# An overflowing expert searched and loaded inside the passes, and the rotary embedding ahead of the norms

## The chip, the core and the metric

The program runs on one core of one Trainium2 chip. A core has TensorE (matmul), VectorE, ScalarE, GpSimd and SyncE, which run side by side and wait for one another by semaphores, and 16 DMA engines, which bring data from HBM to the on-chip memory SBUF. TensorE writes to eight PSUM banks. The metric is device microseconds of one execution; lower is better. All data is float32. [...]

## The reference

256 tokens of width 1024 go through two blocks. The first block has two attentions over one projection and a feed-forward layer. What matters here is its second attention, where queries and keys of 96 per head (64 plain, 32 rotary) are normed and then rotated:

```python
c_q, c_kv, k_rope = ...                       # from proj = rms_norm(x) @ w_in
qb = (rms_norm(c_q, cq_norm_g) @ w_uq).reshape(b, s, 8, 96)
kv = (rms_norm(c_kv, ckv_norm_g) @ w_ukv).reshape(b, s, 8, 128)
kb = concatenate([kv[..., :64], broadcast(k_rope)], -1)
qb, kb = rms_norm(qb, qnorm_b_g), rms_norm(kb, knorm_b_g)
qb = concatenate([qb[..., :64], apply_rope(qb[..., 64:], positions)], -1)   # kb likewise
```

The second block has two layers; each ends with a mixture of 32 experts (1024 to 128 to 1024, gate, up and down), of which every token takes two, and a gated embedding:

```python
hid = silu(einsum('td,edf->tef', xt, w_gate)) * einsum('td,edf->tef', xt, w_up)
y = einsum('tef,efd->td', hid * cw[:, :, None], w_down)    # cw: two non-zero weights for a token
h = h + y
h = h + sigmoid(rms_norm(h, ln_ple) @ ple_w_gate) * (p @ ple_w_proj)
```

Which experts a token takes depends on the data.

## The kernel before

**Weights.** `Stream` loads all weights in the order of use into an arena of 21 buffers of 1 MB (`NB`), on SyncE's queue. `W.room(n)` leaves n buffers to other data; `pump` emits loads while fewer than 21 - n are held and a whole buffer is free; `W.drop` gives one back and pumps. SyncE and TensorE run in the order of the program; VectorE, ScalarE and GpSimd have their orders made by a scheduler, separately inside and outside each branch or loop. A DMA waits on its issuing engine until the one that used the same of eight DMA semaphores before it has landed.

**Products.** Most products are three passes over halves: `split` makes a high part (ScalarE, sometimes GpSimd) and a low part (VectorE, sometimes GpSimd) of each weight, and `mm3` issues three matmuls. In `proj` the split of the next two steps stands ahead of the matmuls, in a ring of five buffers.

**Experts.** In `moe`, eight passes (`q` from 0 to 7, here passes one to eight) take four experts each. Each expert has 32 slots (`CAP`); `pick` makes the selection table `d` of a pass, `gather` collects the tokens, `gate_up`, `hidden`, `turn` and `down` compute, `combine` adds to `acc`. Gate and up are two loads of 0.5 MB for an expert, down one load for two experts. Before pass seven stands the projection of the gated embedding (`ple_proj`). Tokens beyond 32 of an expert are a job: `njob` counts them, and `overflow`, behind pass eight, runs a loop over the jobs inside a branch. In the loop VectorE finds the expert (`top`, `ei`), ScalarE loads the table `c_place` and then the expert's weights by a register, VectorE makes `R.d`, and TensorE gathers and computes up to 112 tokens (`MORE`). In this data the first layer has one job and the second none.

**Second attention of the first block.** The order on TensorE is `cq` (two halves), `ckv`, `qa`, `uq` (two halves), `ukv`, `ka`, `va`, then the transposes `heads_T` to `qTb` and `kTb`. What is made of a product's result (`cq_done`, `ckv_done`, `uq_done`, `ukv_done`, `qkv_done`) is put in `late` and runs two splits into the next product. Behind `ukv` VectorE takes one reciprocal root for q and k together, GpSimd multiplies q by it, and `rope` rotates q and k for each half of the tokens with six VectorE operations; its temporaries come from the ring `sq` of five buffers, which `head_ss` and others share.

**Start.** SyncE issues the identity, `x` in four pieces and the first weights; ScalarE issues `small` (all gains). `Rstd.add` squares a quarter of `h` on ScalarE, and its result `r` is first used in `ckv_done`.

Of the kernel before, what the change touches and what calls it, by code (L numbers as in the profile page):

```python
# [251 lines left out]
def block_kernel(ctx, tc, I, out):  # L252
# [499 lines left out]
    def rope(dst1, dst2, x1, x2, w, t, nh, eng):  # L752
        sh = [128, nh, 16]
        tb = [rt[:, w, i, t].unsqueeze(1).to_broadcast(sh) for i in range(4)]
        uvzy = sq2("ru")[:, 0:64 * nh].rearrange("p (a h d) -> p a h d", a=4, h=nh)
        u, v, z, y = [uvzy[:, i] for i in range(4)]
        eng.tensor_tensor(u, x1, tb[0], OP.mult)
        eng.tensor_tensor(v, x2, tb[1], OP.mult)
        eng.tensor_tensor(z, x2, tb[2], OP.mult)
        eng.tensor_tensor(y, x1, tb[3], OP.mult)  # L760
        eng.tensor_tensor(dst1, u, v, OP.subtract)
        eng.tensor_tensor(dst2, z, y, OP.add)
# [105 lines left out]
    def moe(l, router, rs):  # L868
# [195 lines left out]
        def overflow(T):  # L1064

            gu, dn = take("ovg", [2, 1024]), take("ovd", [1024])
            R = Step(new_d(128), T)
            n = nc.values_load(njob_i[0:1, 0:1], min_val=0, max_val=32)
            with tc.If(n > 0):
                with tc.For_i(0, n, 1):  # L1070
                    tmp = sq2("job")
                    key, hot, cwh = tmp[:, 0:32], tmp[:, 32:64], tmp[:, 64:128].rearrange("p (t q e) -> p t q e", t=2, q=8)
                    top, cnt, keyj = tmp[:, 128:129], tmp[:, 129:130], tmp[:, 130:134].rearrange("p (t a) -> p t a", t=2)
                    wj, place, ei = tmp[:, 134:138].rearrange("p (t a) -> p t a", t=2), tmp[:, 256:384], tmp[:, 138:139]
                    wr = new_d(4)
                    nc.scalar.dma_start(place, I["c_place"])
                    ebase = C("ebase")[:, 0:32]
                    V.tensor_scalar(key, ebase, float(S), None, OP.add)
                    V.scalar_tensor_tensor(hot, jobs, 0.5, key, OP.is_gt, OP.mult)
                    V.tensor_reduce(top, hot, AX.X, OP.max)  # L1080
                    V.tensor_scalar(ei.bitcast(I32), top, 1.0 / S, -1.0, OP.mult, OP.add)
                    e = nc.values_load(ei.bitcast(I32)[0:1, 0:1], engines=(ENG.Activation,), min_val=0, max_val=31)
                    for a, src in enumerate((I["moe_w_gate_2"], I["moe_w_up_2"])):
                        nc.scalar.dma_start(gu[:, a].unsqueeze(1), src[l, bass.ds(e, 1)].rearrange("e (p k) f -> p e (k f)", k=8))
                    nc.scalar.dma_start(dn.unsqueeze(1), I["moe_w_down_2"][l, bass.ds(e, 1)].rearrange("e p n -> p e n"))
                    V.tensor_scalar(hot, key, top, None, OP.is_equal)
                    V.tensor_tensor(key, jobs, hot, OP.mult)
                    V.tensor_reduce(cnt, key, AX.X, OP.add)
                    V.tensor_tensor(jobs, jobs, hot, OP.subtract)

                    V.tensor_scalar(cnt, cnt, float(MORE), float(CAP - MORE + 1 - S), OP.mult, OP.add)
                    V.tensor_tensor(cnt, cnt, top, OP.add)
                    V.tensor_scalar(keyj, k8[:, :, 0:2], cnt, None, OP.subtract)
                    for t in range(2):
                        V.tensor_scalar(R.d[:, t], place, keyj[:, t, 0:1], None, OP.is_equal)
                        V.scalar_tensor_tensor(R.d[:, t], place, keyj[:, t, 1:2], R.d[:, t].bitcast(F32),
                                               OP.is_equal, OP.add)
                    for t in range(2):
                        V.tensor_tensor(cwh[:, t], cw[:, t, :, 0:4], hot.rearrange("p (q e) -> p q e", q=8), OP.mult)
                        V.tensor_reduce(wj[:, t, 0:1], cwh[:, t].rearrange("p q e -> p (q e)"), AX.X, OP.add)  # L1100
                        V.tensor_copy(wj[:, t, 1:2], cw[:, t, 0, 4:5])
                    A.copy(wr[:, :, 0:2], wj)
                    V.tensor_tensor(wr[:, :, 2:4], wj, wr[:, :, 0:2].bitcast(F32), OP.subtract)
                    drain(gather(R.d, [R], R.banks))
                    b = R.bank("ex")
                    for t in range(2):
                        nc.tensor.transpose(b[:, t * 128:(t + 1) * 128], R.d[:, t].bitcast(F32), ident)
                    for t in range(2):
                        mm(b[:, 256:260], R.d[:, t], wr[:, t], start=t == 0, stop=t == 1)
                    A.copy(R.d, b[:, 0:256].rearrange("p (t n) -> p t n", t=2))  # L1110
                    A.copy(R.ej[:, 0], b[:, 256:260])
                    V.tensor_tensor(R.cs, R.ej[:, 0, 0:2], R.ej[:, 0, 2:4], OP.add)
                    V.tensor_scalar(R.cs[:, 0:1], R.cs[:, 0:1], 0.5, None, OP.mult)
                    b = R.gu()
                    for k in range(8):
                        mm(b[:, 0:256], R.xe[:, k], gu[:, :, k * 128:(k + 1) * 128], start=k == 0, stop=k == 7)
                    hidden(R)
                    turn(R)
                    for c in range(2):
                        b = R.bank(f"y{c}")  # L1120
                        mm(b, R.hT, dn[:, c * 512:(c + 1) * 512], start=True, stop=True)
                        A.copy(R.yd[c][:, 0], b)
                        V.tensor_tensor(R.yd[c][:, 1], b, R.yd[c][:, 0].bitcast(F32), OP.subtract)
                    combine(R, False)
            drop("ovg", "ovd")
# [3 lines left out]
        for q in range(8):  # L1129
# [49 lines left out]
        def squares():  # L1179
            for c in range(2):  # L1180
# [75 lines left out]
    for c in range(2):  # L1256
        for t in range(2):
            rs.add(c, t)
# [786 lines left out]
```

## Time and profile before

| | us |
|---|---|
| median of 3 runs | 874.78 (874.02 to 875.28) |
| the profiled execution | 876.18 |
| its span, first to last instruction | 874.4 |
| TensorE busy in it | 824.1 |
| VectorE, ScalarE, GpSimd busy | 520.4, 446.3, 226.0 |

All rows below are of the one profiled execution, with times from the start of its span. PE is TensorE, PEld its loading of the stationary operand, DVE VectorE, ACT ScalarE, POOL GpSimd, SP SyncE; a q behind a name means the engine's sequencer. L995 is line 995 of the kernel. A line of the timeline has start, duration, engine, line, operation, what is written and read, how many, and in brackets the idle time of the engine before it with what ended it.

### The profile page before, as it was taken

To read this page: it belongs to the slowest core of one execution; us is meant where nothing else is said; L and a number is where in the kernel's file an instruction comes from. 1 tells how busy PE (TensorE), PEld (TensorE's weight loads), DVE (VectorE), ACT (ScalarE), POOL (GpSimd) and SP (SyncE) were. 2 spreads that over 40 slices of the span, in tenths; PEclk is the share of its full clock that TensorE was granted. 3 is DMA by queue.
4 is the path that set the end of the run, shared out by engine and by line. 5 is a ranking of instruction groups with operands and counts; after the bars stand their busy time and mean duration, and the time that the engine had idled before them with its cause. 6 is when DMAs were issued, how large, how long until landed. Compare 5 with 4: busy or idle time off the path is not lost. (4 is left out here: it accounts for less than half of the span.)

```text
span 874.4 us, 15706 instructions
## 1 busy us (share of the span) xinstructions
PE 824.1 (94%) x5660; PEld 643.5 (74%) x5660; DVE 520.4 (60%) x1501; ACT 446.3 (51%) x1084; POOL 226.0 (26%) x293
## 2 busy tenths in 40 slices
PE   8997999999999999999899999955899899999997
PEld 5995878999999988686667666625587678666656
DVE  5669666755454567679864644321688875543355
ACT  6675865644444456367764133410676764232463
POOL 2225452222222234314554100000122455000011
PEclk9999999999999999999999999995999899999999
DMA  9991329655556542446024799999363615799971
GB/s 309 385 376 36 128 89 398 241 183 169 197 188 191 193 154 97 147 155 239 4 88 165 284 390 405 408 395 379 133 217 123 221 63 192 285 384 406 408 276 49
DMA packets 85136, 200.04 MB, mean 229 GB/s; under 512 B 5776, under 2 KB 27584, under 8 KB 85056
## 3 DMA queue, kind: packets, MB, share of 16 engines
q1 hardware_dynamic: 82704, 195.61, 61.6%
q10 hardware_dynamic: 2352, 3.40, 1.2%
q8 instruction: 46, 0.75, 0.4%
q14 instruction: 34, 0.28, 0.1%
HBM read 197.93 MB, written 1.06 MB: 228 GB/s over the span
## 5 line engine op out<-in xcount | busy, mean ns | idle before, releaser
L537 DVE TENSOR_TENSOR s<-a,s 128x512 fp32r<-128x512 f32 (+3 forms) x281 | 189.6, 685 | 127.0 <-ACT s L536 92.8
L536 ACT CAST s<-a 128x512 fp32r<-128x512 f32 (+3 forms) x294 | 172.6, 599 | 169.7 <-PE pj L543 71.5
L541 PE MATMUL pj<-s,a 128*128 128x512 f32 (+3 forms) x456 | 176.1, 386 | 4.5 <-ACT a L518 2.9
L542 PE MATMUL pj<-s,a 128*128 128x512 f32 (+3 forms) x456 | 170.6, 374 | 5.5 <-DVE s L537 5.4
L543 PE MATMUL pj<-s,a 128*128 128x512 f32 (+3 forms) x456 | 170.7, 374 | 1.3 <-DVE a L519 1.2
L537 POOL TENSOR_TENSOR s<-a,s 128x512 fp32r<-128x512 f32 (+3 forms) x71 | 90.4, 1273 | 302.8 <-ACT s L536 247.1
L541 PEld LDWEIGHTS pj<-s,a 128*128 128x128 f32 x456 | 86.4, 190 | 23.6 <-issue 5.6
L534 POOL TENSOR_SCALAR s<-a 128x512 fp32r<-128x512 f32 (+3 forms) x58 | 40.5, 698 | 243.0 <-PE pj L543 120.4
L542 PEld LDWEIGHTS pj<-s,a 128*128 128x128 f32 x456 | 86.7, 190 | 19.7 <-DVE s L537 7.4
L543 PEld LDWEIGHTS pj<-s,a 128*128 128x128 f32 x456 | 86.6, 190 | 18.2 <-DVE a L519 3.6
L1517 PE MATMUL f<-a,s 128*128 128x256 f32 x256 | 72.7, 284 | 0.0
L1519 PE MATMUL f<-a,s 128*128 128x256 f32 x256 | 72.4, 283 | 0.0
L1518 PE MATMUL f<-a,s 128*128 128x256 f32 x256 | 72.4, 283 | 0.0
L1027 PE MATMUL gu<-a,xe 128*32 128x256 f32 x1024 | 58.7, 380 | 0.6 <-DVE xe L1002 0.6
L1027 PEld LDWEIGHTS gu<-a,xe 128*32 128x32 f32 x1024 | 32.6, 110 | 28.3 <-issue 4.8
L541 PE MATMUL acc<-s,a 128*128 128x512 f32 x128 | 50.1, 391 | 0.0
L542 PE MATMUL acc<-s,a 128*128 128x512 f32 x128 | 49.9, 390 | 0.0
L543 PE MATMUL acc<-s,a 128*128 128x512 f32 x128 | 49.8, 389 | 0.0
L1517 PEld LDWEIGHTS f<-a,s 128*128 128x128 f32 x256 | 49.1, 192 | 0.2
L1518 PEld LDWEIGHTS f<-a,s 128*128 128x128 f32 x256 | 49.1, 192 | 0.2
L1519 PEld LDWEIGHTS f<-a,s 128*128 128x128 f32 x256 | 49.1, 192 | 0.0
L638 POOL TENSOR_SCALAR P<-P,nd 128x128 f32<-128x128 f32 x64 | 30.9, 495 | 50.8 <-DVE nd L633 18.3
(365 smaller groups left out, 1414.6 us busy)
## 6 DMA issues: line engine op xcount, KB each, us to landing
a<-in_w_ff_dram SPq DMA_DIRECT2D x32, 1024.0 KB, 5.6
a<-in_moe_w_gate_dram SPq DMA_DIRECT2D x64, 512.0 KB, 7.0
a<-in_moe_w_up_dram SPq DMA_DIRECT2D x64, 512.0 KB, 8.2
a<-in_moe_w_down_dram SPq DMA_DIRECT2D x32, 1024.0 KB, 9.2
a<-in_a_w_in_dram SPq DMA_DIRECT2D x10, 1024.0 KB, 5.1
a<-in_ple_w_gate_dram SPq DMA_DIRECT2D x8, 1024.0 KB, 15.6
a<-in_w_in_dram SPq DMA_DIRECT2D x6, 1024.0 KB, 14.8
a<-in_w_o_dram SPq DMA_DIRECT2D x4, 1024.0 KB, 14.2
```

Of the source, the lines that this page charges most:

```text
L534: G.tensor_scalar(hi, wv, 1.0, 0.0, OP.mult, OP.add)
L536: A.copy(hi, wv)
L537: (G if nsplit[0] % 5 == 2 else V).tensor_tensor(lo, wv, hi.bitcast(F32), OP.subtract)
L541: mm(ps, xh, hi, start=st, stop=False)
L542: mm(ps, xh, lo, start=False, stop=False)
L543: mm(ps, xl, hi, start=False, stop=sp)
L638: G.tensor_scalar(p[:, o0:o0 + n], p[:, o0:o0 + n], rc[:, t, i:i + 1], 1.0, OP.mult, OP.mult)
L1027: mm(b[32 * e:32 * e + 32, 0:256], T.xe[:, k, 32 * e:32 * e + 32], w, start=k == 0, stop=k == 7)
L1517: mm(o, hi[:, fs], xt[0][:, k], start=st, stop=False)
L1518: mm(o, hi[:, fs], xt[1][:, k], start=False, stop=False)
L1519: mm(o, lo[:, fs], xt[0][:, k], start=False, stop=sp)
```

## The change

Four things change.

1. `overflow` becomes a class. It is made in pass four: it takes its buffers, ScalarE issues the load of the table, and VectorE's search (`find`) follows. In pass five SyncE reads the expert from a register and issues its three loads (`load`), in both layers, whether there is a job or not (expert 0 then); all engines read the number of jobs there. Behind pass eight VectorE makes the table (`pick`) ahead of a branch for more than 0 jobs, which holds the computation once (`run`); a second branch for more than 1 holds a loop with search, loads, table and computation. `W.room(4)` stands from pass three on.
2. `rope` works on both halves of a rotary part at once, with three operations, and moves ahead of the norms: k into `ckv_done` (both halves of the tokens in one call), q into `uq_done`. q and k take their roots separately (`rsqrt_b`), and q is multiplied in `uq_done`. The transposes to `qTb` are woven into `ka`.
3. The first two pieces of `x` go by ScalarE's queue ahead of `small`.
4. The squares and the root `r` of the first norm stand behind the first half of `cq`.

```diff
-    nc.scalar.dma_start(small, I["c_small"])
     for c in range(2):
         for t in range(2):
-            nc.sync.dma_start(h[:, t, c * 512:(c + 1) * 512], I["x"][0, t * 128:(t + 1) * 128, c * 512:(c + 1) * 512])
+            (nc.sync if c else nc.scalar).dma_start(h[:, t, c * 512:(c + 1) * 512],
+                                                    I["x"][0, t * 128:(t + 1) * 128, c * 512:(c + 1) * 512])
+        if not c:
+            nc.scalar.dma_start(small, I["c_small"])
         W.room(NB - 1 - 2 * c)
...
-    def rope(dst1, dst2, x1, x2, w, t, nh, eng):
...
+    def rope(dst, x, tb):
+
+        n = x.shape[1]
+        u, v = sq2("ru")[:, 0:64 * n].rearrange("p (w h a d) -> w p h a d", w=2, a=2, d=16)
+        V.tensor_tensor(u, x, tb[0], OP.mult)
+        V.tensor_tensor(v, x[:, :, ::-1], tb[1], OP.mult)
+        V.tensor_tensor(dst, u, v, OP.add)
...
-        def overflow(T):
...
+        class Overflow:
...
+            def __init__(self):
+                self.gu, self.dn = take("ovg", [2, 1024]), take("ovd", [1024])
+                f = take("ovf", [512])
...
+                nc.scalar.dma_start(self.place, I["c_place"])
+                self.find()
+
+            def find(self):
...
+                V.tensor_scalar(self.ei, top, 1.0 / S, 1.0, OP.mult, OP.max)
...
+            def load(self):
+                e = nc.values_load(self.ei[0:1, 0:1], engines=(ENG.SP,), min_val=1, max_val=32) - 1
+                for a, src in enumerate((I["moe_w_gate_2"], I["moe_w_up_2"])):
+                    nc.sync.dma_start(self.gu[:, a].unsqueeze(1),
+                                      src[l, bass.ds(e, 1)].rearrange("e (p k) f -> p e (k f)", k=8))
+                nc.sync.dma_start(self.dn.unsqueeze(1), I["moe_w_down_2"][l, bass.ds(e, 1)].rearrange("e p n -> p e n"))
...
+            def all(self, T, n):
+                R = Step(new_d(128), T)
+                self.pick(R.d)
+                with tc.If(n > 0):
+                    self.run(R)
+                with tc.If(n > 1):
+                    with tc.For_i(1, n, 1):
+                        self.find()
+                        self.load()
+                        self.pick(R.d)
+                        self.run(R)
+                drop("ovg", "ovd", "ovf")
...
+            if q == 2:
+                W.room(4)
+            if q == 3:
+                over = Overflow()
+            if q == 4:
+                over.load()
+                njob_r = nc.values_load(njob_i[0:1, 0:1], min_val=0, max_val=32)
             if q == 5:
-                W.room(4 if l else 9)
+                W.room(6 if l else 9)
...
-        overflow(T)
+        over.all(T, njob_r)
...
-    for c in range(2):
-        for t in range(2):
-            rs.add(c, t)
     drain(xt_feats(hsrc, 0, 4, [(xt, "mix", 0)]))
-    r = rs.get()
-    r2 = st(2)
-    V.tensor_tensor(r2, r, r, OP.mult)
...
     drain(proj(xt, "cq", 384, cq_done(0),
                mid=xt_feats(hsrc, 4, 8, [(xt, "mix", 0)])))
+    for c in range(2):
+        for t in range(2):
+            rs.add(c, t)
+    r = rs.get()
+    r2 = st(2)
+    V.tensor_tensor(r2, r, r, OP.mult)
...
+        kv = kr.rearrange("p t (a d) -> p t a d", a=2)
+        rope(kv, kv, [rt[:, 1, i] for i in range(2)])
...
+    def rsqrt_b(i):
+        xb = tiny.tile([128, 32], F32, tag="xb", name="xb", bufs=1)[:, 0:16]
+        V.tensor_scalar(xb, ssq[:, i].rearrange("p t h -> p (t h)"), 1.0 / 96, EPS, OP.mult, OP.add)
+        rsqrt(rsb[:, i].rearrange("p t h -> p (t h)"), xb, 16)
...
+            if c:
+                for t in range(2):
+                    qv = qbr[:, t, :, 64:96].rearrange("p h (a d) -> p h a d", a=2)
+                    rope(qv, qv, [rt[:, 0, i, t].unsqueeze(1).to_broadcast([128, 8, 2, 16]) for i in range(2)])
+                rsqrt_b(0)
+                for t in range(2):
+                    G.tensor_tensor(qbr[:, t], qbr[:, t], rsb[:, 0, t].unsqueeze(2).to_broadcast([128, 8, 96]), OP.mult)
...
-    rsqrt(rsb.rearrange("p a t h -> p (a t h)"), xb, 32)
+    rsqrt_b(1)
...
-    drain(kproj)
+    qTb = take("qTb", [8, S])
+    weave(kproj, heads_T(qTb, lambda t, f: qbr[:, t, f], 8, 96, qsc[:96, 1:2]), 0.7, -1.0)
```

## Rows read from the trace of the kernel before

**Rows 1.** The page, part 1: busy time, share and instructions of each engine.

```profile
PE 824.1 (94%) x5660; PEld 643.5 (74%) x5660; DVE 520.4 (60%) x1501; ACT 446.3 (51%) x1084; POOL 226.0 (26%) x293
```

**Rows 2.** Timeline from the first layer's pass eight through the overflowing expert.

```profile
580.76 1.92 PE L1047 MATMUL y<-a,hd 128*32 128x512 f32 x16 [0.35 <-ACT hd L1041]
...
592.93 0.34 ACTq L1076 DMA_DIRECT2D job<-in_c_place_dram  x1
...
598.29 0.48 DVE L1095 TENSOR_SCALAR d<-job 128x128 fp32r<-128x128 f32 x2 [11.56 <-DMA job<-in_c_place_dram]
...
599.18 7.06 PE L995 MATMUL ov<-d,a 128*128 128x128 f32 x32 [16.49 <-DVE d L1096]
...
606.76 5.18 PE L1116 MATMUL ov<-a,xe 128*128 128x256 f32 x16
```

**Rows 3.** Stretches: busy of PE, PEld, DVE, ACT, POOL; clock, DMA share, GB/s.

```profile
84.13:90.95 6.82, 6.06 (x17) 4.79 (x18) 5.54 (x15) 1.34 (x3) 2.30 (x2) 0.50 0.00 0
...
585.89:609.78 23.89, 10.60 (x43) 10.10 (x44) 3.12 (x17) 1.77 (x7) 0.00 (x0) 0.50 1.05 380
684.20:688.29 4.09, 2.20 (x15) 1.60 (x15) 3.73 (x13) 2.05 (x4) 0.01 (x1) 1.00 0.79 262
688.29:695.11 6.82, 6.25 (x29) 4.32 (x29) 4.68 (x26) 4.94 (x20) 0.78 (x2) 0.50 0.44 136
...
540.00:575.00 35.00, 32.86 (x309) 22.55 (x311) 11.08 (x32) 14.46 (x35) 1.28 (x1) 1.00 1.03 408
770.00:832.00 62.00, 59.80 (x610) 40.14 (x612) 23.60 (x74) 22.10 (x55) 0.62 (x1) 1.00 1.02 403
```

**Rows 4.** Timeline of TensorE: one gather, and pass eight's gate and up, either layer.

```profile
551.49 4.08 PE L995 MATMUL g<-d,a 128*128 128x256 f32 x32
...
574.62 3.64 PE L1027 MATMUL gu<-a,xe 128*32 128x256 f32 x64
...
832.64 3.64 PE L1027 MATMUL gu<-a,xe 128*32 128x256 f32 x64
```

**Rows 5.** Line 320: issue and landing of the last up weights, pass eight.

```profile
L320 SPq DMA_DIRECT2D a<-in_moe_w_up_dram x1: 328/328/328, 564.0 to 564.0; - x1
...
L320 SPq DMA_DIRECT2D a<-in_moe_w_up_dram x1: 328/328/328, 821.3 to 821.3; - x1
...
DMA to landing us min/median/max: 10.2/10.2/10.2
```

**Rows 6.** Timeline of the first block's second attention, between `ukv` and `va`.

```profile
65.78 0.42 DVE L604 TENSOR_REDUCE stage<-sq 128x4 f32<-128x256 f32 x1 [1.13 <-ACT sq L603]
...
76.22 3.86 POOL L1424 TENSOR_TENSOR a<-a,stage 128x768 f32<-128x768 f32 x2 [0.81 <-DVE stage L479]
...
78.67 1.55 DVE L757 TENSOR_TENSOR ru<-a,stage 128x128 f32<-128x128 f32 x1
...
84.16 0.68 DVE L537 TENSOR_TENSOR s<-a,s 128x512 fp32r<-128x512 f32 x1
...
84.89 0.79 PE L542 MATMUL pj<-s,a 128*128 128x512 f32 x1 [5.01 <-DVE s L537]
```

**Rows 7.** Timeline of the start.

```profile
1.18 0.90 SPq L392 DMA_DIRECT2D a<-in_x_dram  x2
...
7.38 0.51 ACT L536 CAST s<-a 128x384 fp32r<-128x384 f32 x1 [4.90 <-DMA a<-in_w_in_dram]
...
8.32 0.44 PE L541 MATMUL pj<-s,a 128*128 128x384 f32 x1 [1.12 <-ACT a L518]
...
17.12 0.45 PE L543 MATMUL pj<-s,a 128*128 128x384 f32 x1 [0.63 <-DVE a L519]
```

**Rows 8.** Timeline of the second layer's end, behind the branch.

```profile
840.91 2.10 PE L1058 MATMUL acc<-yd,d 128*128 128x512 f32 x8 [0.18 <-PEq L1069]
```

More of the change, by code (lines that the diff above doesn't have):

```diff
@@ L750, in __call__ @@
             return v
-    def rope(dst1, dst2, x1, x2, w, t, nh, eng):
[L753 to L762, printed above, removed]
+    def rope(dst, x, tb):
[4 more added lines that the diff above has]
+        V.tensor_tensor(dst, u, v, OP.add)
     def load_wr(l):
@@ L1062, in combine @@
                         (A.copy if t else V.tensor_copy)(h[:, t, c * 512:(c + 1) * 512], acc[t][c])
-        def overflow(T):
[L1066 to L1093, printed above, removed]
-                    for t in range(2):
[L1095 to L1118, printed above, removed]
-                    for c in range(2):
[L1120 to L1125, printed above, removed]
@@ L1255, in block_kernel @@
     rs = Rstd("r1")
-    for c in range(2):
-        for t in range(2):
-            rs.add(c, t)
     drain(xt_feats(hsrc, 0, 4, [(xt, "mix", 0)]))
-    r = rs.get()
-    r2 = st(2)
-    V.tensor_tensor(r2, r, r, OP.mult)
     ssx = st(8)
@@ L1276, in block_kernel @@
                mid=xt_feats(hsrc, 4, 8, [(xt, "mix", 0)])))
+    for c in range(2):
+        for t in range(2):
+            rs.add(c, t)
+    r = rs.get()
+    r2 = st(2)
+    V.tensor_tensor(r2, r, r, OP.mult)
     pf = tiny.tile([128, 2], F32, tag="pf", name="pf")
@@ L1298, in block_kernel @@
     A.activation(cs, kk, AF.Sin)
-    rt = st(2, 4, 2, 16)
+    rt = st(2, 2, 2, 2, 16)
     for w in range(2):
@@ L1303, in block_kernel @@
         g2 = small[:, ro + 16:ro + 32].unsqueeze(1).to_broadcast([128, 2, 16])
-        V.tensor_tensor(rt[:, w, 0], cs, g1, OP.mult)
-        V.tensor_tensor(rt[:, w, 1], sn, g2, OP.mult)
-        V.tensor_tensor(rt[:, w, 2], cs, g2, OP.mult)
-        V.tensor_tensor(rt[:, w, 3], sn, g1, OP.mult)
+        V.tensor_tensor(rt[:, w, 0, :, 0], cs, g1, OP.mult)
+        V.tensor_tensor(rt[:, w, 0, :, 1], cs, g2, OP.mult)
+        V.scalar_tensor_tensor(rt[:, w, 1, :, 0], sn, -1.0, g2, OP.mult, OP.mult)
+        V.tensor_tensor(rt[:, w, 1, :, 1], sn, g1, OP.mult)
     vps = bank("vps")
@@ L1379, in f @@
                 head_ss(ssq[:, 0, t, 4 * c:4 * c + 4], pv_, 4, 96, rqk[:, t:t + 1])
+            if c:
+                for t in range(2):
+                    qv = qbr[:, t, :, 64:96].rearrange("p h (a d) -> p h a d", a=2)
+                    rope(qv, qv, [rt[:, 0, i, t].unsqueeze(1).to_broadcast([128, 8, 2, 16]) for i in range(2)])
+                rsqrt_b(0)
+                for t in range(2):
+                    G.tensor_tensor(qbr[:, t], qbr[:, t], rsb[:, 0, t].unsqueeze(2).to_broadcast([128, 8, 96]), OP.mult)
         return f
@@ L1416, in block_kernel @@
         V.tensor_scalar(ssq[:, 1, t], ssq[:, 1, t], sskr[:, t:t + 1], None, OP.add)
-    xb = tiny.tile([128, 32], F32, tag="xb", name="xb", bufs=1)
-    V.tensor_scalar(xb, ssq.rearrange("p a t h -> p (a t h)"), 1.0 / 96, EPS, OP.mult, OP.add)
-    rsb = st(2, 2, 8)
-    rsqrt(rsb.rearrange("p a t h -> p (a t h)"), xb, 32)
+    rsqrt_b(1)
     kbr = take("kbr", [2, 8, 96])
-    krr = st(2, 32)
     for t in range(2):
-        G.tensor_tensor(qbr[:, t], qbr[:, t], rsb[:, 0, t].unsqueeze(2).to_broadcast([128, 8, 96]), OP.mult)
-        rope(qbr[:, t, :, 64:80], qbr[:, t, :, 80:96], qbr[:, t, :, 64:80], qbr[:, t, :, 80:96], 0, t, 8, V)
-        rope(krr[:, t, 0:16].unsqueeze(1), krr[:, t, 16:32].unsqueeze(1),
-             kr[:, t, 0:16].unsqueeze(1), kr[:, t, 16:32].unsqueeze(1), 1, t, 1, V)
         V.tensor_tensor(kbr[:, t, :, 0:64], kvb[:, t, :, 0:64],
                         rsb[:, 1, t].unsqueeze(2).to_broadcast([128, 8, 64]), OP.mult)
-        G.tensor_tensor(kbr[:, t, :, 64:96], krr[:, t].unsqueeze(1).to_broadcast([128, 8, 32]),
+        G.tensor_tensor(kbr[:, t, :, 64:96], kr[:, t].unsqueeze(1).to_broadcast([128, 8, 32]),
                         rsb[:, 1, t].unsqueeze(2).to_broadcast([128, 8, 32]), OP.mult)
@@ L1451, in block_kernel @@
         next(vproj)
-    qTb = take("qTb", [8, S])
     kTb = take("kTb", [8, S])
-    drain(heads_T(qTb, lambda t, f: qbr[:, t, f], 8, 96, qsc[:96, 1:2]))
     drain(heads_T(kTb, lambda t, f: kbr[:, t, f], 8, 96, gain("kb", 0, 96)))
-    drop("qbr", "kbr")
+    drop("kbr")
     qTa = take("qTa", [4, S])
```

49 lines of the change are left out of this document (added).

## The prediction

> **What bounds the kernel now.** I read the page first, then the waits of TensorE from the longest down, then the timeline around each, then the stretches at half clock, and last SyncE's order of weight loads. TensorE is busy for 94% of the span [rows 1], so only work taken from it, or its idle stretches, can shorten the run. Two idle stretches are long, and the change touches both.
>
> The first ends the first expert layer. TensorE finishes pass eight at 582.7 and stands for 16.49 us until `R.d` is built [rows 2]. The reader should see the chain in those rows. The table `c_place` is issued by ScalarE only at 592.93, VectorE waits 11.56 us for it, and its two picks release TensorE at 599.18. The granted clock is 0.50 from 585.89 to 609.78 [rows 3], so the gather and the expert's gate and up products behind the idle run at half speed too. In the second layer no expert overflows: TensorE waits 0.18 us at the branch [rows 8].
>
> The second is in the first block. TensorE waits 5.01 us for a weight split that VectorE makes at 84.16, behind the rotary embedding that starts at 78.67, and then runs 6.06 busy us at half clock [rows 3, 6].
>
> A third place is no loss yet. Late in both expert layers the DMA engines are full (403 to 408 GB/s) [rows 3], and the last gate and up weights of pass eight arrive just in time: issued at 564.0 and 821.3, they land 10.2 us later, at 574.2 and 831.5, for products that start at 574.62 and 832.64 [rows 4, 5]. That is 0.4 and 1.1 us of slack.
>
> **The change part by part.**
>
> *Overflow in the first layer.* The search, the table and the three loads move to passes four and five, the picks ahead of the branch, and the loop goes. The 16.49 us of idle vanish but for a branch, for which I take the 0.18 us of rows 8. Without idle the clock stays up. The gather, 32 products in 7.06 us, then costs what the same line costs for 32 products of twice the columns for passes seven and eight, 4.08 us; gate and up, 5.18 us, what one pass takes for as many columns, 3.64 us [rows 2, 4]. Together 16.49 - 0.18 + 2.98 + 1.54 = 20.8 us gained. If the half clock stays, only 16.3 are gained; the small products in between could bring the upper end to 21.5. I take 20.8, since the rows at full clock are from the same layer. The picks themselves are under work: VectorE is busy for 11.08 of 35 us there [rows 3].
>
> *The loads in pass five.* They now go out in both layers, also where nothing overflows, and SyncE issues them in the order of the program. I counted `Stream`: with room(4) from pass three on, 41 items are out when pass five begins, which is up to the gate and up weights of pass seven. The three loads (0.52 MB each) therefore stand ahead of the down weights of pass seven and of all weights of pass eight. At 408 GB/s they take 3.9 us from DMA engines that are full, so the weights of pass eight land 3.9 us later. Against the slack, TensorE waits 3.5 us in the first layer and 2.8 in the second: 6.3 us lost. The two buffers that the stream gives up cost nothing, as the loads wait there for the DMA engines and not for buffers; if they did, every buffer would be released within a pass. Bounds: 0 (the DMA engines catch up elsewhere) and 7.8 (no slack).
>
> Other work queues in front of this wait and is covered by it: the search on VectorE, the register load on TensorE, and ScalarE, which may stand at the issue of the table until an earlier transfer is done, as it did until 592.93. What delays TensorE in passes four to seven by less than 3 us only shortens the wait in pass eight; without that cover it would be paid in full.
>
> [...]
>
> *The clock in those waits.* An idle of 5.01 us was followed by half clock, and so was a stretch of 4.09 us in which TensorE worked for 2.20 [rows 3, 6]. New waits of 3.5 and 2.8 us lie between these two. What a fall costs is half of the 6.06 busy us at 84.13: 3.0. I take one fall in the two layers, 3.0; bounds 0 and 6.0.
>
> [...]
>
> *Rotary embedding.* Six VectorE operations for each half of the rows, for q and for k, become three, and they move ahead of the norms: k into `ckv_done`, q into `uq_done`. Nothing of them is left between 76 and 85 us. That takes away the 5.01 us of idle and the 3.0 us of half clock: 8.0. Against that, six operations of 256 elements at 0.42 us, the row of that size [rows 6], or 2.5 us, go where VectorE's idle is 1.13 us at 65.78; 1.4 us are late for the weight splits of `ka`. GpSimd's two multiplies of q, 3.86 us, also move forward to where it makes splits, and the transposes of q now wait for them inside `ka`. I charge 1.5 in all; bounds 0 and 5.4. Net gain 6.5, from 2.6 to 8.0.
>
> *The start.* SyncE issues its first weight 0.90 us earlier, since the two first pieces of `x` go by ScalarE's queue [rows 7]. TensorE's first product waits 1.12 us behind the first split, which waits for that weight [rows 7], so up to 0.9 is gained. The squares of `rs.add` leave the feature transposes; the wait of 0.63 us at 17.12 is of that kind, and I take 0.5. Sum 1.4; bounds 0 and 1.75. The squares later lie beside `cq` and `ckv` products.
>
> *Second branch.* One more compare on each engine in both layers; 0.18 us each [rows 8], 0.4 together; bounds 0 and 1.
>
> **Sum.** -20.8 - 6.5 - 1.4 + 6.3 + 3.0 + 0.4 = -19.0. The profiled execution took 876.18 us (span 874.4), so 857.2; the median of the runs is 874.78, which lies 1.4 lower, and on that basis 855.8 us.
>
> **The rivals.**
>
> *No fall, or two.* 852.8 with no fall, 858.8 with two. For none speaks that the waits are shorter than 5 us; for two, that 1.9 us of idle within 4.09 was enough once.
>
> *The loads are hidden.* If pass eight doesn't wait, the 6.3 and the 3.0 go: 846.5. Against it stands the 0.4 us of slack under full DMA engines.
>
> *The norm of q takes the place of the rotary embedding.* GpSimd multiplies before it splits, and VectorE's backlog moves to 68 us: the net gain is the lower bound, 2.6 instead of 6.5: 859.7.
>
> *The change doesn't do what it says.* The picks or the table come late and TensorE stands at the branch for some 5 us, with the clock down behind it: 5 + 4.5 more, 865.3. The table is ordered some 50 us ahead, which speaks against it.
>
> *SyncE stands (slower than before).* SyncE's register load waits for VectorE's search, and every later weight is queued behind it. Transfers in flight last 10.2 us [rows 5]. If the search came more than that after SyncE arrives, both layers would stop. It ends slower than before when each layer loses 9.5 us, a search some 20 us late. VectorE is mostly free and the search is ordered a pass ahead; I give it little.
>
> **How the numbers follow.** One fall, 855.8: 0.36. No fall: 0.18. Two: 0.16. Loads hidden: 0.11. Norm of q: 0.08. Picks late: 0.06. SyncE stands: 0.05. The range from 846 to 866 leaves out the last and small parts of the others. A measurement can tell a change of about 0.2% (1.7 us) from none; all but the last case lie beyond it, with 0.02 between: faster 0.93, same 0.02, slower 0.05.
>
> **What would show it.** Right: TensorE's wait ahead of `ov` under 1 us and full clock there; the three moe loads on SyncE before the down weights of pass seven in both layers; a wait of 3 to 4 us on a DMA at pass eight of both layers; no wait of 5 us near 80 and full clock there; the first product before 7.6. Wrong: pass eight without a wait, long waits of ScalarE at the table's issue in pass four that TensorE feels, or TensorE standing at q's transposes in `ka`.

## The result, and the profile after

The changed kernel takes 863.39 us (median of four runs, 859.88 to 865.36), the kernel before 875.03 in the runs beside it: a ratio of 0.9865 with a 95% interval of 0.9835 to 0.9896, so it is 11.6 us or 1.35% faster. The forecast was 855.8, range 846 to 866. The profiled execution is the fastest of the four, 859.88 (span 858.0), 16.3 below the profiled one of before; the forecast, on that basis, was 857.2.

Cut at events that both kernels have, the 16.4 us of span come out like this (us):

| stretch, by events of TensorE | before | after | change | forecast |
|---|---|---|---|---|
| span's start to the first expert layer's router | 482.24 | 477.88 | -4.36 | -7.9 (start, rotary embedding) |
| router to the end of pass eight, first layer | 100.45 | 106.30 | +5.85 | +3.5, and a clock fall of 3.0 in one of the layers |
| there to the first product behind the transposes | 40.66 | 19.67 | -20.99 | -20.6 |
| there to the second layer's router | 116.89 | 114.71 | -2.18 | 0 |
| router to the end of pass eight, second layer | 100.49 | 103.07 | +2.58 | +2.8 |
| there to the end | 33.67 | 36.37 | +2.70 | +0.2 |

The page of the changed kernel, its part 1 and, from part 3, the queue of the kind instruction, whose 47 packets, here called fetches, have 16,384 bytes each in the trace:

```profile
PE 819.1 (95%) x5660; PEld 638.4 (74%) x5660; DVE 523.0 (61%) x1520; ACT 445.5 (52%) x1085; POOL 224.4 (26%) x293
...
q8 instruction: 47, 0.77, 0.4%
```

The stretches at half clock (0.50 granted; the clock records of both profiles hold 0.50 and 1.00 and no other value), and the late passes (columns as in [rows 3]):

```profile
72.70:76.11 3.41, 3.41 (x10) 2.63 (x9) 3.41 (x9) 0.62 (x1) 1.01 (x1) 0.50 0.01 2
530.08:536.91 6.83, 6.11 (x37) 2.62 (x41) 2.56 (x10) 1.81 (x4) 0.00 (x0) 0.50 1.04 407
827.04:830.46 3.42, 3.42 (x13) 2.93 (x12) 2.26 (x5) 2.60 (x7) 0.00 (x0) 0.50 0.30 108
...
540.00:575.00 35.00, 32.86 (x299) 23.17 (x301) 11.95 (x35) 13.99 (x34) 1.28 (x1) 1.00 1.03 409
```

The 23.89 us at half clock behind the overflow search [rows 3] are gone, and so is the stretch at 688, behind a wait of 1.52 us that both kernels have. That one is the -2.18 of the table and is not to be credited to the change: the program is the same there, and five kernels built on the change (e3, e5, e6, e8, e9) show half clock in that place again, for 3.4 to 6.8 us. Three other stretches stand in the change; the first takes the place of the one at 84.

The timeline of TensorE from pass eight through the overflowing expert, which answers to [rows 2, 4]:

```profile
576.10 3.64 PE L1025 MATMUL gu<-a,xe 128*32 128x256 f32 x64
...
582.26 1.92 PE L1045 MATMUL y<-a,hd 128*32 128x512 f32 x16 [0.35 <-ACT hd L1039]
584.11 3.79 PE L993 MATMUL ov<-d,a 128*128 128x128 f32 x32
...
588.13 3.70 PE L1128 MATMUL ov<-a,xe 128*128 128x256 f32 x16
```

The gather starts as pass eight ends: the 16.49 us are gone. The gather takes 3.79 us and gate and up 3.70, where 4.08 and 3.64 were forecast.

Pass eight shows no wait in the first layer. Here is line 320 in two windows, the issue of its last up weights in either layer, and for the second layer who waited for them:

```profile
L320 SPq DMA_DIRECT2D a<-in_moe_w_up_dram x1: 328/328/328, 563.6 to 563.6; - x1
...
L320 SPq DMA_DIRECT2D a<-in_moe_w_up_dram x1: 328/328/328, 803.2 to 803.2; - x1
...
  PE gu L1025: 0.3, 1
...
DMA to landing us min/median/max: 10.2/10.2/10.2
```

They land at 573.8 and 813.4. Counted from the router of their layer that is 4.0 and 3.6 us later than before [rows 5]: what the forecast took for the three loads, 3.9. But in the first layer TensorE comes to pass eight 5.8 us late already, for this (timeline of SyncE, ScalarE and TensorE up to pass four):

```profile
516.64 0.38 SPq L803 DMA_DIRECT2D ple_p<-in_p_dram  x1
...
528.87 0.33 ACTq L1077 DMA_DIRECT2D a<-in_c_place_dram  x1
529.24 0.19 ACT L1099 CAST wr<-a 128x4 fp32r<-128x4 f32 x1 [5.99 <-DMA ple_p<-in_p_dram]
...
530.80 0.48 PE L1038 MATMUL ht<-ident_r,hd 128*128 128x128 f32 x1 [2.76 <-DVE hd L1034]
```

ScalarE stands 5.99 us at its issue of the table, until a load that SyncE issued 12 us earlier has landed; in the trace both transfers count on the same DMA semaphore, 107, one of the eight that its DMAs use. Behind it waits the activation of pass four, behind that VectorE, and behind that TensorE: 2.76 us of wait, and 6.11 busy us at half clock, 5.8 in all. In the second layer the same chain has a wait of 1.40 and leaves the clock alone. Counted from the router, TensorE is 1.7 us late there behind pass four, and 0.9 more behind pass eight's gate and up, where the late weights do bind.

The second attention of the first block, which answers to [rows 6] (timeline of GpSimd, VectorE, TensorE):

```profile
68.47 2.90 POOL L1425 TENSOR_TENSOR a<-a,stage 128x768 f32<-128x768 f32 x2 [6.79 <-ACT sq L605]
...
69.34 0.63 DVE L1462 TENSOR_SCALAR stage<-stage 128x8 f32<-128x8 f32 x1
...
70.32 1.07 DVE L1462 TENSOR_SCALAR stage<-stage 128x8 f32<-128x8 f32 x1
71.31 0.68 DVE L539 TENSOR_TENSOR s<-a,s 128x512 fp32r<-128x512 f32 x1
...
72.04 0.50 PE L544 MATMUL pj<-s,a 128*128 128x512 f32 x1 [2.52 <-DVE s L539]
```

A wait of 2.52 us with 3.41 at half clock stands where 5.01 and 6.82 stood: 8.0 was to go, and half of it went.

The start, which answers to [rows 7]:

```profile
1.18 0.42 SPq L299 DMA_DIRECT2D a<-in_w_in_dram  x1
...
7.95 0.44 PE L543 MATMUL pj<-s,a 128*128 128x384 f32 x1 [0.81 <-ACT a L520]
...
23.08 0.44 PE L544 MATMUL pj<-s,a 128*128 128x384 f32 x1 [1.05 <-DVE s L539]
...
39.70 0.60 PE L503 MATMUL tps<-ident_r,a 128*128 128x128 f32 x4
```

The first product is 0.37 earlier, and the transposes at 39.7 start when they did before (39.69): nothing is left of the 1.4 forecast.

The end of the second layer, which answers to [rows 8]:

```profile
822.24 1.16 PE L1056 MATMUL acc<-yd,d 128*128 128x512 f32 x4 [0.61 <-PEq L1143]
826.09 1.08 PE L1056 MATMUL acc<-yd,d 128*128 128x512 f32 x4 [2.69 <-ACT s L538]
```

The combine, eight products in one run before, breaks in the middle for 2.69 us, and half clock follows. The releaser that the row names makes no sense (a split of a weight that the product doesn't read). The forecast did not have this stand.

### The profile page after: what moved, and what is told of

Same layout as the page of the kernel before. It is cut to its first block, busy times and chain, and to the rows that moved or that the text cites. A ratio compares the mean times of both kernels' runs of the same rounds, so it can differ in the third digit from the quotient of the medians.

```text
span 858.0 us, 15691 instructions
## 1 busy us (share of the span) xinstructions
PE 819.1 (95%) x5660; PEld 638.4 (74%) x5660; DVE 523.0 (61%) x1520; ACT 445.5 (52%) x1085; POOL 224.4 (26%) x293
## 5 line engine op out<-in xcount | busy, mean ns | idle before, releaser
L539 DVE TENSOR_TENSOR s<-a,s 128x512 fp32r<-128x512 f32 (+3 forms) x281 | 189.7, 685 | 120.4 <-ACT s L538 86.4
L539 POOL TENSOR_TENSOR s<-a,s 128x512 fp32r<-128x512 f32 (+3 forms) x71 | 89.5, 1261 | 316.5 <-ACT s L538 290.1
```

What stands on the lines that cost most here:

```text
L539: (G if nsplit[0] % 5 == 2 else V).tensor_tensor(lo, wv, hi.bitcast(F32), OP.subtract)
```

## The experiments

All are compared with runs of the kernel before on the same chip (medians 875.0 to 875.5).

| | median, us | ratio to before, 95% |
|---|---|---|
| the change | 863.39 | 0.9865 [0.9835, 0.9896] |
| e1 overflow alone | 869.48 | 0.9940 [0.9926, 0.9954] |
| e2 rotary embedding alone | 871.03 | 0.9951 [0.9937, 0.9964] |
| e3 table by SyncE | 864.88 | 0.9880 [0.9865, 0.9895] |
| e4 short second body | 861.29 | 0.9850 [0.9835, 0.9865] |
| e5 branch sooner | 860.76 | 0.9833 [0.9812, 0.9854] |
| e6 loads behind | 855.04 | 0.9759 [0.9742, 0.9775] |
| e7 one body | 875.81 | 1.0000 [0.9991, 1.0010] |
| e8 norm of q by VectorE | 866.15 | 0.9883 [0.9865, 0.9900] |
| e9 longer unused body | 864.02 | 0.9866 [0.9843, 0.9890] |
| e10 loads last | 853.72 | 0.9744 [0.9728, 0.9761] |
| e11 squares back | 851.12 | 0.9725 [0.9712, 0.9738] |
| e12 all mended | 848.61 | 0.9696 [0.9680, 0.9711] |

**e1 and e2: the parts alone.** The kernel before with only the lines of the overflow, or only those of the rotary embedding and the norms.

> The kernel before with the overflow part of the change alone (search in pass four, loads in pass five, two branches); start and rotary embedding as before. The forecast's terms for this part sum to -20.8 + 6.3 + 3.0 + 0.4 = -11.1, 865.1 on the profiled run of before. Reading of the changed kernel's trace: 20.7 gained between the two layers, but 5.8 lost in passes four to eight of the first layer, 2.6 in those of the second and 4.0 behind the second layer's branches: -8.3, 867.9. If the parts don't act on each other, the change less this run and less the rotary embedding leaves nothing for the start.

> The kernel before with the rotary embedding and the norm of q moved, nothing else. The forecast's main case: -6.5, 869.7, no wait over 1 us near 75. The rival named in the forecast (the norm of q takes its place): -2.6, 873.6, with a wait for a VectorE split near 70. Reading of the changed kernel's trace: a wait of 2.5 us stays at 70, with 3.4 us of half clock behind it, -4.0, 872.2.

The overflow alone gives 5.9, the rotary embedding 4.3; together they give 10.2 of the whole's 11.6. The intervals, over 1 us to either side each, show no sign that the parts act on each other. For e2 the reading of the trace holds and the forecast's main case is out: a wait of 2.50 us near 70 stays, this time without half clock behind it. e1 gave less than both its forecasts: the gaps of the last combine (2.77) and of pass four (2.24) come back, and another stands behind the overflow with 3.53 us, where the profiled execution of the change has 1.28.

**e3: the table off ScalarE's queue.**

```diff
-                nc.scalar.dma_start(self.place, I["c_place"])
+                nc.sync.dma_start(self.place, I["c_place"])
```

> The changed kernel with one word altered: the table c_place is issued by SyncE and not by ScalarE. Theory: ScalarE stands 6.0 us at this issue in pass four (4.8 in the second layer) and TensorE feels 2.8 and 1.4 us of it, with the half clock behind the first. Both waits go in every case. If the weights of pass eight bind next, landing 3.9 us later for the three loads as the forecast has it, TensorE then waits at pass eight: only 2.3 us are gained in the first layer (its products start 2.3 us after the last weight lands now) and about nothing in the second: -2.3, 857.6 against the profiled 859.9. If the weights don't bind, all of 5.8 and 1.4 comes back: -7.2, 852.7, with no wait on a DMA at pass eight.

The waits of pass four go in both layers, and the forecast's waits appear at pass eight. These are the sum of TensorE's waits for the up weights, the timeline of pass eight of either layer, and ScalarE and TensorE behind the overflow:

```profile
PE gu L1025 <- DMA a<-in_moe_w_up_dram: 3.9, 2, 2.0
...
573.55 3.61 PE L1025 MATMUL gu<-a,xe 128*32 128x256 f32 x58 [1.96 <-DMA a<-in_moe_w_up_dram]
...
603.02 0.47 ACT L520 ACTIVATE a<-tps,small 128x256 fp32r<-128x256 f32 x1 [2.96 <-SPq L1143]
...
603.55 0.79 PE L543 MATMUL pj<-s,a 128*128 128x512 f32 x1 [3.57 <-ACT a L520]
...
818.50 3.61 PE L1025 MATMUL gu<-a,xe 128*32 128x256 f32 x58 [1.96 <-DMA a<-in_moe_w_up_dram]
```

So the cover is shown: ScalarE's stall hid the late weights, 1.96 us of wait in each layer. With the products slowed beside the wait (the six ahead of it take 1.12 and 1.21 us, the 58 behind it 3.61), pass eight ends 3.1 and 3.2 us later after its router than in the kernel before; the forecast had 3.5 and 2.8. The 2.6 us that TensorE still won in the first layer were gone at 603.55: it waits there for ScalarE, and ScalarE for SyncE at line 1143, the second branch. The median, 864.88, is no better than the change's, so neither the -2.3 nor the -7.2 expected came.

**e5: SyncE at the branch sooner.** To e3, in the first layer:

```diff
+            if q == 7 and not l:
+                W.room(13)
...
         over.all(T, njob_r)
+        if not l:
+            W.room(9)
```

> The kernel of the run before last but one (table by SyncE) with the room of the weight stream cut from 12 to 8 buffers in pass eight of the first layer and given back behind the branches: four loads of 1 MB that SyncE issued ahead of the branches are issued behind them. Theory: in the run with the table by SyncE, TensorE won 2.6 us in the passes and lost them again at 600, in a wait of 3.57 us for ScalarE, which waits for SyncE to pass the second branch (at 603.0 in both kernels, whenever the others are there); SyncE gets there late because it is held at its loads by the full DMA engines. With four loads fewer ahead of it SyncE is there by 592: the wait falls to the 0.5 to 1.3 us of before, and the 6.8 us of half clock behind it go: -2.5 to -6, from 864.9 to between 859 and 862. Rival, ScalarE waits there for a weight or a buffer: the wait stays, 864.9. The waits of 1.96 us at pass eight stay in both layers.

SyncE's instructions of line 1143 in the changed kernel and, second, in e5; third, ScalarE and TensorE of e5 there:

```profile
L1143 SPq COMPARE_BRANCH  x1: 50/50/50, 602.4 to 602.4; - x1
```

```profile
L1143 SPq COMPARE_BRANCH  x1: 50/50/50, 588.9 to 588.9; - x1
```

```profile
602.14 0.48 ACT L520 ACTIVATE a<-tps,small 128x256 fp32r<-128x256 f32 x1
602.67 0.50 PE L543 MATMUL pj<-s,a 128*128 128x512 f32 x1 [0.51 <-ACT a L520]
```

With four loads of 1 MB fewer in front of it SyncE passes 13.5 us sooner than in the change (13.2 sooner than in e3), the wait of 3.57 is 0.51, and the median is 4.1 us lower than e3's, as expected. In the kernels with the change's first block and its two branches that leave these loads in front (the change, e3, e4, e8, e9) SyncE passes at 601.6 to 602.9, and the products behind the transposes start between 603.0 and 604.4, while TensorE's end of pass eight moves by 3.2 us. In the first layer it was SyncE, held at its loads, that set the time: in the change four issues of 1 MB take it 10.92 us from 578.15, with the DMA engines full (1.05 and 382 GB/s from 575.0 to 602.4).

**e6 and e10: the three loads later.** Both are e5 with the loads moved. In e6 `over.load()` stands at the head of pass seven, behind all gate and up weights; in e10 it stands behind the last down weights too, and e9's edit is in. The move in e6:

```diff
             if q == 6:
+                over.load()
                 combine(prev, False)
...
             if q == 4:
-                over.load()
```

> The kernel with fewer loads ahead of the branches, and the three loads of the overflowing expert moved from pass five to pass seven, behind all gate and up weights of pass eight. Theory, the forecast's: the loads take 3.9 us of full DMA engines ahead of those weights; without them the wait of 1.96 us at pass eight goes in both layers: -3.9 against the run beside it, 855 to 858. The expert's weights land some 5 us ahead of their products (at 578 against 584 or later). Rival: the weights of pass eight are late for another reason (the reissue of buffers): the waits stay. Second rival: the expert's weights now come late, and a wait stands ahead of its gate and up products.

> The kernel with table by SyncE and fewer loads ahead of the branches; the three loads stand behind all weights of pass eight, the last down weights too; and the unused body of the run beside it is in. Theory: against the run with the loads ahead of the last down weights (855.0 median, 854.8 profiled) the wait of 1.07 us for these weights in the first layer goes, and so do the gap of 3.1 us behind the branches of the second layer and its half clock: -1.1 - 3.1 - 1.7 = -5.9, 849 profiled. Rival: the expert's weights land late now, behind 1.5 MB more, and a wait of 1 to 4 us stands ahead of its gate and up products: 850 to 853. Second rival: the gap in the second layer stays, 853.7.

In e6 both waits at pass eight are gone, and the median is 5.7 us below e5's: the two waits, and half clock for 3.4 us that e5 has behind the first of them. A wait of 1.07 us for the first layer's last down weights (2.1 us with the slower products beside it) is the only trace of the loads. In e10 that goes too, and pass eight ends 100.5 us after its router in both layers, as in the kernel before. The expert's weights are in time in both kernels. So the price of the three loads, and its place, were as forecast; it fell due only where nothing hid it. e10's profile, 850.3, has the gap of e6's last combine no more but another wait behind it, which is told under e12.

**e4 and e9: the gap in the last combine.** e4 takes the call of `run` out of the loop behind the second branch; e9 makes that body longer, in the first layer alone.

```diff
                         self.run(R)
+                        if l == 0:
+                            warm(90, R.bank("y0"))
```

> The changed kernel without the call of run in the loop behind the second branch (a loop that these inputs never enter), so that the branch that skips it jumps over some 110 instructions of TensorE fewer. Theory, instruction fetch: in the second layer TensorE jumps over both bodies, past what its queue has fetched, and stands 2.7 us in the middle of the last combine until the next block of instructions is there. With the shorter jump the gap of 2.7 us and the half clock behind it (1.7) go: -2.7 to -4.5, 855.4 to 857.2. Rival, the branch itself or the table of splits behind it costs this: the gap stays, 859.9.

> The changed kernel with 90 products of constants added at the end of the loop behind the second branch, in the first layer alone: 180 instructions of TensorE that these inputs never execute. Nothing that runs is altered. Theory, instruction fetch: TensorE's instructions come in blocks of 256, and after the jump in the second layer TensorE executes only some 14 before it crosses into a block whose fetch began at the jump. The 180 instructions shift the program against the blocks, so that some 80 instructions follow the jump in its block: the gap of 2.7 us and the half clock behind it go, -2.7 to -4.5, 855.4 to 857.2 on the profiled 859.9. Rival, the length of the jump or the branch itself costs it: the gap stays in the second layer, and the first layer, which now jumps farther, may show one too: 859.9 to 864.

[rows 8] as they are in e9, and what follows:

```profile
828.37 2.08 PE L1056 MATMUL acc<-yd,d 128*128 128x512 f32 x8 [0.61 <-PEq L1143]
830.86 0.33 PE L503 MATMUL tps<-ident_r,a 128*128 128x128 f32 x1 [0.41 <-DVE a L1060]
```

The gap is gone in both, in e9 by instructions that are never executed and belong to the other layer. The medians can't show it (e4's is 2.1 us below the change's, within the spread of the two); the profiles do. From the end of pass eight to the end of the span the six kernels with the gap (the change, e1, e3, e5, e6, e8) take 36.3 to 37.6 us, e9 34.5, e4 33.9 and the kernel before 33.7: the gap is worth some 1.9 to 2.5 us. In e6 the row says plainly that TensorE waited for nothing that the profile shows:

```profile
820.24 2.72 PE L1056 MATMUL acc<-yd,d 128*128 128x512 f32 x6 [3.14 <-issue]
```

Start and duration of the q8 fetches around it, from the trace's records of that queue, and the end of TensorE's last branch instruction (with two branches, the second):

```
before   837.69 1.13   846.36 1.11                 jump at 839.5
change   813.99 1.11   823.60 1.11   827.55 1.16   jump at 822.1
e9       810.73 1.11   822.58 1.11   829.57 1.05   jump at 828.2
```

In the change TensorE jumps, runs half a combine, and stands until 826.09, 1.4 us after the end of a fetch that began only after the jump. It is so in all six kernels with the gap: such a fetch begins 1.4 to 1.6 us after the second jump, and the gap ends 1.3 to 1.5 us after the fetch. In e9 a fetch had begun 5.6 us ahead of the jump and was done 4.5 ahead of it, and the combine runs through. That this fetch brought the combine's block is worked out from the order of the fetches; the records don't name what a fetch brings. The 256 instructions of e9's expectation agree with the traces: over the first 24 fetches TensorE starts 257 on average from one fetch to the next in the change (202 to 333), and 258 in the kernel before, with the weight loads, semaphore and branch instructions counted. From the second jump to the gap the change's trace has ten, where 14 were expected; the 80 no record shows. e9 jumps as far as the change in the second layer and has no gap, so it isn't the length of the jump alone that decides. That it is the place of the code behind the jump in the blocks is my reading of e4 and e9, and is not shown. All the same, e9's median is no better than the change's. Its profiled execution shows the wait for SyncE with 3.39 us, and half clock from 602.1 and from 670.4, 6.83 us each.

**e7: one body for both cases.**

```diff
-                    self.run(R)
-                with tc.If(n > 1):
-                    with tc.For_i(1, n, 1):
-                        self.find()
...
+                    with tc.For_i(0, n, 1) as i:
+                        with tc.If(i > 0):
+                            self.find()
...
                         self.run(R)
```

> The changed kernel with one branch and one loop instead of two branches: the first round of the loop runs the expert already found, a branch inside it finds and loads the next one for later rounds; there is one body to jump over, as before the change. Theory, instruction fetch: the gap of 2.7 us in the last combine of the second layer goes with the half clock behind it, -2.7 to -4.5; the end of the loop in the first layer costs 0 to 3 back. 855 to 860 against the profiled 859.9. Rival: the loop's end is dearer than the second branch, slower than the changed kernel.

The rival's outcome holds, though not by the loop's end that it named. The gap in the second layer goes, but in the first layer the expert's own products now wait until SyncE, which may load their weights there, has passed the inner branch, and the whole gain of the change is lost:

```profile
584.69 7.06 PE L993 MATMUL ov<-d,a 128*128 128x128 f32 x32 [2.54 <-DVEq L1143]
603.95 5.92 PE L1128 MATMUL ov<-a,xe 128*128 128x256 f32 x16 [11.52 <-SPq L1143]
```

SyncE gets there at 603.2, again behind its queue of loads.

**e8: q's norm by VectorE.** `G.tensor_tensor` becomes `V.tensor_tensor` in the two multiplies of `uq_done`.

> The changed kernel with the two multiplies that norm q done by VectorE and not by GpSimd. Theory, contention: while GpSimd runs them (2.9 us at 68.5), VectorE's small operations of 16 columns take 0.58 to 1.21 us, not 0.17, and the split that TensorE waits for 2.5 us stands behind these; with the multiplies on VectorE (some 0.9 us each) the wait at 70 falls below 1.5 us: -1 to -3. Rival, the plain backlog of VectorE: 1.8 us more work in front of that split, the wait grows to 3.5 to 4.3 us and half clock follows: +1 to +3.

```profile
68.70 1.83 DVE L1425 TENSOR_TENSOR a<-a,stage 128x768 f32<-128x768 f32 x2
...
71.54 0.23 DVE L1462 TENSOR_SCALAR stage<-stage 128x8 f32<-128x8 f32 x1
...
73.01 0.50 PE L544 MATMUL pj<-s,a 128*128 128x512 f32 x1 [3.48 <-DVE s L539]
```

The longer operations are there: the 128x8 operation takes 0.23 us, not 0.63 and 1.07 as beside GpSimd's multiplies. In the change its two runs end at 69.97 and 71.39, within 0.03 us of the ends of the two multiplies (69.94 and 71.37), while the 128x256 reductions beside them take 0.41 us with and without GpSimd. The operations of 16 columns that the expectation names, 0.58 and 1.21 us, start later in the change, at 71.91 and 72.53, beside GpSimd's next split (71.33 to 73.71); in e8, where GpSimd does nothing at that time, they take 0.17 and 0.18. What lengthens these and not the reductions isn't shown. But some 1.2 us saved against 1.83 more work is a loss: the wait grows by 1.0, as the rival had it. VectorE's backlog is what TensorE waits for.

**e11 and e12: the squares, and the end of the second layer.** e11 is e10 with `rs.add` back in the feature transposes; e12 is e11 with the loads of the second layer where e6 has them.

> The run beside it with the squares of rs.add back in the feature transposes, ahead of the first products, as before the change; x still comes by two queues. Forecast: the move of the squares was worth 0.5 us, so this is 0.5 slower. Reading of the changed kernel's trace: the move gained 1.85 us by the product vps (18.25, before 20.10) and gave it all back in two waits for VectorE splits at 19.4 and 22.0 and slower products behind them, so that the transposes at 39.7 start at the same time in both kernels: with the squares back those waits go, and the transposes near 40 start up to 1 us earlier than 39.7 or at the same time: -1 to 0.

> The run with the squares back, with one line moved: in the second layer the three loads stand where they were two steps before (ahead of the last down weights of pass eight); in the first layer they stay behind them. In the run with the squares back (851.1 median, 850.8 profiled) TensorE waits 3.3 us at 814.6 for VectorE, which splits two weights of the next stage before it copies the sum of the experts out of PSUM; that order came from the place of the loads, and with the loads moved VectorE copies first, as in the changed kernel. Theory: that wait falls to about 0.9 (as with the longer unused body) and the half clock behind it goes: -2.4 - 1.7, 846.7 profiled, 847 to 849 median. Rival: the loads now hold up the second layer's last down weights and a wait of 1 us comes back there, or VectorE is late for another reason: 850 to 852.

The transposes near 40 in e10 and, second, e11:

```profile
39.79 0.60 PE L503 MATMUL tps<-ident_r,a 128*128 128x128 f32 x4
```

```profile
39.18 0.60 PE L503 MATMUL tps<-ident_r,a 128*128 128x128 f32 x4
```

The move of the squares costs some 0.5 us: the nine profiles that have it and `x` by two queues put these transposes at 39.5 to 39.9, e11 and e12 at 39.2 and 39.3. `x` by two queues gains about as much (39.69 before): the start's two edits cancel. In e10 and e11 TensorE waits 3.3 us behind the last combine, since VectorE splits two weights (L539) before it copies the sum out (L1060). VectorE and TensorE in e10, with the wait, and, second, in e12, without:

```profile
814.85 1.95 DVE L539 TENSOR_TENSOR s<-a,s 128x512 fp32r<-128x512 f32 x2 [2.03 <-ACT s L538]
816.73 0.68 DVE L1060 COPY a<-acc 128x512 f32<-128x512 f32 x1
...
817.46 1.10 PE L503 MATMUL tps<-ident_r,a 128*128 128x128 f32 x8 [3.31 <-DVE a L1060]
```

```profile
814.56 0.69 DVE L1060 COPY a<-acc 128x512 f32<-128x512 f32 x1 [0.98 <-PE acc L1056]
...
815.30 0.33 PE L503 MATMUL tps<-ident_r,a 128*128 128x128 f32 x1 [0.35 <-DVE a L1060]
816.11 0.98 PE L503 MATMUL tps<-ident_r,a 128*128 128x128 f32 x7 [0.48 <-ACT a L1060]
```

Why the place of the loads alters VectorE's order isn't shown. e12 is 26.8 us faster than the kernel before and its median is 14.8 below the change's: the gain is more than twice the change's.

## Why the prediction was right or wrong

The sign and the main term were right, and the total came out 7.6 us above the likeliest value by the medians, 2.7 by the profiles. That it came so near owes something to luck: the step for the loads has nearly the right size from another cause, and 2.18 us of the profiled gain lie in a stretch that the change doesn't touch.

- *Overflow, 20.8.* Right: 21.0, with the clock up, and gather and gate and up at the prices read from the same layer at full clock. The 21.0 include the wait of 1.28 us at the stretch's end.
- *The loads, 6.3, and one fall of the clock, 3.0.* Late weights were the right mechanism, and e3 and e6 show it, but in the change they weren't what cost most of the time. The weights landed 4.0 and 3.6 us late (3.9 forecast). Of the waits at pass eight, "3.5 us in the first layer and 2.8 in the second", the first didn't come and the second came as 0.9, because TensorE had lost 5.8 and 1.7 us in pass four already. The forecast had that stall, that ScalarE "may stand at the issue of the table", but counted it as covered: a delay of less than 3 us "only shortens the wait in pass eight". With the fall of the clock behind it, it passed that limit in the first layer. That 9.3 forecast stands against 8.4 in the table is therefore luck, and two of the forecast's own signs of being wrong were there: pass eight without a wait in the first layer, and a stall of ScalarE at the table's issue that TensorE feels. Where the stall is taken away (e3) the loads cost 3.1 and 3.2 us, which is the 6.3 priced but for 0.1.
- *Rotary embedding, 6.5.* Mis-sized: it gave 4.0 by the product `cmph` at 350.66 (354.64 before), and 5.2 by the same product in e2's profile, where no half clock follows the wait. The third rival had the mechanism: VectorE's backlog moved to 68 us. The 5.01 us became 2.5, and the charge of 1.5 should have been 4.
- *Start, 1.4.* Mis-sized: 0.0. The term for the first queue was 0.5 and not 0.9; the squares, 0.5 gained in the forecast, cost about 0.5 (e11, e12).
- *Second branch, 0.4 with bounds 0 and 1.* Failed: TensorE stood 2.69 us and ran 3.4 us at half clock, 2.7 us net in the table. The price was read from a branch over one body [rows 8]; the row couldn't show what comes behind two bodies, the gap of 2.69 us that e4 and e9 don't have.
- *What was missing: SyncE's way to the branch.* The forecast looked at SyncE's register load and found it harmless, and no row shows a wait there; it didn't ask when SyncE, with twelve loads for later stages queued in front of the branches, would get there. The 16.49 us of idle had hidden that. As long as SyncE passes near 602.4, what TensorE gains in the first layer's passes is worth nothing (e3). How much of that time is due to the three loads, which stand in the same queue, no run shows.

The other three runs of the change are 2.4 to 5.5 us slower than the profiled one, and no trace of them was kept. The mean granted clock of the two slowest is 0.983 and 0.987, of the profiled one 0.992. By my estimate from these that is some 15 and 9 us more at half clock, which at half of that time lost is enough for the 5.5 and most of the 4.7 us. The third, 2.4 us slower, has 0.994, so there the clock is not the reason; a longer wait for SyncE, as in e9's profile (3.39 us against 1.28), could be, which is argued and not shown.

## What to carry to other kernels

When a long idle stretch goes, list what it was hiding on every engine, the issuing ones too: here ScalarE, and TensorE behind it, waited at a branch for SyncE, the last to reach it. So keep loads of the next stage behind the join. A small DMA on a compute engine's queue can stop that engine until somebody else's transfer lands (5.99 us of ScalarE here); put it on the queue of the engine that is waiting for DMA anyway, and put optional loads behind those with a due time. A skipped body is not always free: behind the second one of the change TensorE stood 2.69 us, and behind a shorter one (e4), or with instructions added that never run (e9), it didn't; so read the trace behind the jump, also where nothing is executed. And when a total comes out near the forecast, check each term against its own stretch: one term here had the right size for the wrong reason.

## What the runs showed of the hardware

- Behind two jumps TensorE ran four products in the change, stood 2.69 us, and went on 4.0 us after the second jump (822.1 to 826.1), with a fetch of 1.1 us in between; in the six kernels with the gap it was 4.0 to 4.1. The jump itself showed as an idle of 0.18 us over one body (before, e2, e7) and of 0.61 with two branches (the change, e9).
- A DMA issue stood 5.99 us on ScalarE until a transfer issued by SyncE had landed, and 4.63 in the second layer.
- The same wait of 2.50 to 2.52 us near 70 was followed by 3.41 us at half clock in eight of the kernels with the new norms, and by none in e2, e4 and e10. The wait alone doesn't decide it; what does isn't shown. One program differs from execution to execution: e10 took 850.3 and 850.5 us at a mean granted clock of 0.997, and 853.7 to 854.1 at 0.991. This is why differences of 2 us here need the rows and not the medians.
